# Decay weights of the state-space branch: the clipped difference formed by ScalarE, then one exponent of eight heads

## The chip, the cores and the metric

The kernel runs on one core of a Trainium2 chip. The metric is the device time of one execution in microseconds (us): the kernel before takes 2112.63 us, the median of three runs (2110.53 to 2113.01).

The engines are called PE (TensorE: matmuls and transposes), DVE (VectorE), ACT (ScalarE), POOL (GpSimd) and SP (SyncE, which issues the DMAs). PEld is the loading of PE's weights. Each engine takes its instructions strictly in the order in which they were written for it; an instruction that waits holds up all that stand behind it on its engine.

## The reference

A trunk of two layers. Each layer normalises its 1088 tokens (a prompt of 1024 and a sample of 64), projects them by one matrix, and sends column groups of the result through three branches: A, a gated linear recurrence; B, sparse attention, whose 256 keys per query are picked by an indexer score; C, a state-space scan (SSD). The three outputs are concatenated, projected back and added to the input. What the change touches lies in branch C:

```
cum   = cumsum(dt * a)                       # per chunk of tokens, per head
seg   = cum[l] - cum[s]
decay = exp(where(s <= l, seg, -inf))
wts   = decay * (C[l] . B[s]) * dt[s]
y     = wts @ x + (C @ h_prev) * exp(cum[l]) # and the state h moves on from chunk to chunk
```

## The kernel before

All tokens are worked on in chunks of 384, 384 and 320 columns, features on the partitions. A projection of 128 features is 72 matmuls (three per block of 128 inputs, since weights and activations are each split into a high and a low part, lines 235 to 237), and its weights are split by ACT (line 212, `whi`) and by POOL or DVE (line 213, `wlo`).

In the middle of each layer several things run side by side, and a plan string (`PLAN`) says in what order the program writes them:

- the projections for the state-space branch (`xbc`), each followed by a convolution of four taps (ACT line 872, POOL, DVE line 878), a tanh on ACT (line 887) and a product on DVE (line 888); gates (ACT line 431, DVE line 432); later the projections of branch A (`lru`);
- the selection of the keys (`select`), a binary search over the 31 bits of a threshold. Per bit DVE forms a candidate (line 622), DVE counts three score tiles against it (line 596), ACT counts four (line 602, `junka`), and DVE compares and keeps (lines 629 and 630). One bit is written after each projection, at a later priority;
- the scan (`ssd`), in 18 steps per layer (two head groups of eight heads, nine token tiles of 128 or 64). `ssd_inputs` prepares a step one step ahead of its use.

`ssd_inputs` loads the cumulative sums of eight heads, spread over all partitions, into `cumB` (partition: token s; columns: eight heads by 128 tokens l; DMA at line 730; two buffers). Then come eight DVE instructions, one per head, that subtract the head's column of `ctk` (cum[s], one number per partition) and cut at zero (line 760); one ACT exponent over all eight heads (line 763); one DVE product with the masked `C.B` (line 764). The result is the moving side of the 16 small matmuls at line 811, whose outputs DVE adds up (lines 807, 814, 815, 822). The inputs `xsc`, `bc` and `eB` of a step are DMAs too (lines 726, 728, 735), and PE transposes `xsc` at line 750.

The order of the instructions on each engine isn't the order of the program text. A scheduler places them by its own estimate of when each is ready, with the plan's order as priority, so that a change of one operation moves others. Buffers and semaphores follow from that order.

Of the kernel before, what the change touches and what calls it, by code (L numbers as in the profile page):

```python
# [14 lines left out]
AF = mybir.ActivationFunctionType  # L15
OP = mybir.AluOpType
# [56 lines left out]
def rows_of(t):  # L73
    return 128 if t < 8 else TS
# [14 lines left out]
def body(ctx, tc, I, O):  # L89
    nc = tc.nc  # L90
    V, G, S, PE, SP = nc.vector, nc.gpsimd, nc.scalar, nc.tensor, nc.sync

    def dram(x, off, ap):
        return bass.AP(tensor=x.tensor, offset=x.offset + off, ap=ap)
# [28 lines left out]
    def tp_bank():  # L123
        return bank("tp", 2)
# [175 lines left out]
    for l in range(DEPTH):  # L300
# [31 lines left out]
        with ExitStack() as st:  # L332
# [16 lines left out]
            for ci, (a, b) in enumerate(CH):  # L349
# [6 lines left out]
                for d in range(8):  # L356
# [3 lines left out]
                    else:  # L360
# [3 lines left out]
                                           op0=OP.mult, op1=OP.mult)  # L364
# [13 lines left out]
        dt, ctk, te, dec = [one.tile([128, NT, 16], F32, name=n) for n in ("dt", "ctk", "te", "dec")]  # L378
# [64 lines left out]
        g = nq = hl = None  # L443
# [28 lines left out]
        with ExitStack() as st:  # L472
# [38 lines left out]
            for j, zn in zip((6, 5, 4, 3, 2, 1, 0), IZ):  # L511
                fill(zn)
                t = j + 2
                n = rows_of(t)
# [14 lines left out]
                for c0 in range(0, nks[j], 512):  # L529
                    c1 = min(c0 + 512, nks[j])  # L530
                    for h in range(4):
# [5 lines left out]
                        if h == 0:  # L537
# [5 lines left out]
                                               op0=OP.mult, op1=OP.add)  # L543
# [20 lines left out]
            for t0, t1 in ((0, 4), (4, 8), (8, 9)):  # L564
                ps = tp_bank()
                w = 0
                for t in range(t0, t1):
                    n = rows_of(t)
# [148 lines left out]
        def ssd_inputs(g, tt):  # L717


            p = sa  # L720
            n = rows_of(tt)
            tok = tt * 128
            pad = tok + (3 if tt == 8 else 0)
            g8 = slice(8 * g, 8 * g + 8)
            xsc = p.tile([128, 4, 128], F32, name="xsc")
            SP.dma_start(xsc[:, :, :n], xsd[g][:, :, pad:pad + n])
            bc = p.tile([128, 2, 128], F32, name="bc")
            SP.dma_start(bc[:, :, :n], xsd[2][:, g:g + 3:2, pad:pad + n])
            cumB = p.tile([128, 8, 128], F32, name="cumB")
            SP.dma_start(cumB[:n, :, :n], cumd[None, g8, tok:tok + n].to_broadcast([n, 8, n]))  # L730
            eB = None
            if tt:
                eB = p.tile([128, 4, 128], F32, name="eB")
                for b in range(2):
                    SP.dma_start(eB[64 * b:64 * b + 64, :, :n],
                                 dram(cumd, (8 * g + b) * T + tok, [[0, 64], [2 * T, 4], [1, n]]))
                S.activation(eB[:, :, :n], eB[:, :, :n], AF.Exp)
            B_, C_ = bc[:, 0, :n], bc[:, 1, :n]

            ps = tp_bank()  # L740
            PE.matmul(ps[:n, :n], B_, C_, start=True, stop=True)
            PE.transpose(ps[:n, 128:256], B_, ident)
            cbm = p.tile([128, 128], F32, name="cbm")
            V.tensor_tensor(cbm[:n, :n], ps[:n, :n], triu[:n, :n], op=OP.mult)
            bt = p.tile([128, 128], F32, name="bt")
            S.activation(bt[:n], ps[:n, 128:256], AF.Copy)

            ps = tp_bank()
            for i in range(4):
                PE.transpose(ps[:n, i * 128:(i + 1) * 128], xsc[:, i, :n], ident)  # L750
            pv = ps[:n].rearrange("p (h c) -> p h c", h=8)
            xdt = p.tile([128, 8, 64], F32, name="xdt")
            V.tensor_tensor(xdt[:n], pv, dt[:n, tt, g8][:, :, None].to_broadcast([n, 8, 64]), op=OP.mult)
            xde = p.tile([128, 8, 64], F32, name="xde")
            G.tensor_tensor(xde[:n], xdt[:n], te[:n, tt, g8][:, :, None].to_broadcast([n, 8, 64]), op=OP.mult)
            G.tensor_tensor(xsc[:, :, :n], xsc[:, :, :n], dcol[:, 4 * g:4 * g + 4][:, :, None].to_broadcast([128, 4, n]),
                            op=OP.mult)

            for h in range(8):
                V.tensor_scalar(cumB[:n, h, :n], cumB[:n, h, :n], ctk[:n, tt, 8 * g + h:8 * g + h + 1], 0.0,  # L760
                                op0=OP.subtract, op1=OP.min)
            cB = cumB[:n, :, :n]
            S.activation(cB, cB, AF.Exp)
            V.tensor_tensor(cB, cB, cbm[:n, None, :n].to_broadcast([n, 8, n]), op=OP.mult)  # L764
            return xsc, C_, eB, bt, xdt, xde, cB

        def ssd(g):
            p = sa
            hT = None
            g8 = slice(8 * g, 8 * g + 8)  # L770
            order = [0, 1, 2, 3, 4, 5, 8, 6, 7]
            ready = ssd_inputs(g, 0)
            for k, tt in enumerate(order):
                ci = min(tt // 3, 2)
# [5 lines left out]
                if k + 1 < len(order):  # L780
                    ready = ssd_inputs(g, order[k + 1])
# [153 lines left out]
        g = [ssd(0), ssd(1)]  # L935
# [316 lines left out]
```

## Time and profile before

| | |
|---|---|
| median of 3 runs | 2112.63 us |
| profiled execution: its own time | 2118.68 us |
| its span | 2116.9 us |
| mean granted clock of PE | 0.98 |
| busy: PE, PEld, DVE, ACT, POOL | 93%, 84%, 76%, 54%, 31% |

The profiled execution is 6.05 us above the median. All times of the trace are from it. PE's busy share is modelled, and high all over; the shares of the other engines are means over stages that differ, so the stage in which the change lies has to be looked at by itself.

### The profile page before, as it was taken

The numbers are of one execution on the slowest core, as the hardware profiler recorded it, in microseconds if no ns is written. First come the engines' busy times: TensorE is split into PE (matmuls) and PEld (weight loads), VectorE is DVE, ScalarE is ACT, GpSimd is POOL, SyncE is SP. The second block draws the span as 40 slices with busy tenths as digits, with TensorE's granted clock in tenths as the row PEclk, the third lists the DMA queues.
The fourth block names the chain that finished last, engine by engine and source line by source line (L and its number), as shares of the span: only waits on it lengthen the run. The fifth ranks groups of instructions, "written<-read, shape, count | busy, mean of one in ns | idle before, by whom it ended". The sixth has DMA issues, their size and how long they took to land.

```text
span 2116.9 us, 34794 instructions
## 1 busy us (share of the span) xinstructions
PE 1975.6 (93%) x12076; PEld 1767.8 (84%) x12076; DVE 1614.3 (76%) x4102; ACT 1132.9 (54%) x2244; POOL 654.5 (31%) x561
## 2 busy tenths in 40 slices
PE   5989989888999899999999999988899998999999
PEld 5889988878898788866998999887888897888589
DVE  8668999999886875475287889999998778556723
ACT  5558967622465454445255798664324565444521
POOL 3012243433332332142430222443334225223420
PEclk9999999999999999999999999999999998999999
DMA  4135353353533642332641343534454326334145
GB/s 137 55 64 155 95 143 119 101 172 104 139 90 101 208 143 90 107 100 88 199 143 55 94 116 101 161 106 127 118 153 119 118 104 207 108 91 131 57 132 171
DMA packets 253368, 255.11 MB, mean 121 GB/s; under 512 B 31048, under 2 KB 233192, under 8 KB 253192
## 3 DMA queue, kind: packets, MB, share of 16 engines
q1 hardware_dynamic: 253192, 252.89, 39.9%
q8 instruction: 95, 1.56, 0.3%
q14 instruction: 81, 0.66, 0.1%
HBM read 176.68 MB, written 76.14 MB: 119 GB/s over the span
## 4 chain that ended last, share of the span: by engine, by line
PE 51%; DVE 29%; DMA 9%; issue 5%; ACT 3%; SPq 1%; POOL 1%; DVEq 0%; ACTq 0%; POOLq 0%
PE mm L236 12%; PE mm L237 12%; PE mm L235 11%; PE s L1119 4%; PE tp L1114 3%; PE s L1089 3%; DVE junk L596 3%; DVE u L878 3%; DMA cumB<-cumd 3%; DVE cumB L760 3%; DMA biasd<-g 2%; PE s L534 1%; PE s L904 1%; ACT junka L602 1%; DVE cumB L764 1%
## 5 line engine op out<-in xcount | busy, mean ns | idle before, releaser
L213 POOL TENSOR_TENSOR wlo<-wraw,whi 128x1024 fp32r<-128x1024 f32 x80 | 198.1, 2476 | 390.8 <-ACT whi L212 378.1
L602 ACT ACTIVATE junka<-sc,cand 128x768 bf16<-128x768 f32 x248 | 239.1, 966 | 24.7 <-DVE cand L622 20.6
L212 ACT ACTIVATE whi<-wraw 128x1024 fp32r<-128x1024 f32 x130 | 137.1, 1054 | 148.1 <-PE mm L236 89.3
L1096 ACT ACTIVATE lg<-lg,mx 128x512 f32<-128x512 f32 (+8 forms) x144 | 111.3, 773 | 108.8 <-DVE mx L1092 108.0
L1081 POOL TENSOR_TENSOR nbm<-nb,shared 128x256 f32<-128x256 f32 (+1 forms) x112 | 81.3, 729 | 231.1 <-DVE mx L1092 208.9
L878 DVE SCALAR_TENSOR_TENSOR u<-raw,parh,u 128x384 f32<-128x384 f32 (+1 forms) x198 | 144.7, 736 | 1.9 <-ACT u L872 0.8
L1116 ACT ACTIVATE pT<-tp 128x512 f32<-128x512 f32 (+1 forms) x164 | 90.2, 568 | 101.8 <-PE tp L1114 99.9
L596 DVE TENSOR_SCALAR_CACHE_REDUCE junk<-sc,cand 128x384 bf16<-128x384 f32 (+4 forms) x194 | 140.1, 752 | 0.7
L1089 PE MATMUL s<-kst,qst 128*128 128x512 f32 (+4 forms) x448 | 120.6, 361 | 9.7 <-DVE mx L1092 9.3
L1114 PEld LDWEIGHTS tp<-identr,lg 128*128 128x128 f32 (+2 forms) x656 | 71.8, 140 | 46.9 <-issue 39.7
L1114 PE MATMUL tp<-identr,lg 128*128 128x128 f32 (+2 forms) x656 | 107.3, 278 | 0.7 <-DVE lg L1099 0.7
L1119 PE MATMUL s<-pT,vt 128*64 128x256 f32 (+2 forms) x656 | 103.9, 392 | 1.6 <-ACT pT L1116 1.6
L1099 DVE TENSOR_SCALAR lg<-lg,ri 128x512 f32<-128x512 f32 (+8 forms) x144 | 98.1, 681 | 3.5
L760 DVE TENSOR_SCALAR cumB<-cumB,ctk 128x128 f32<-128x128 f32 (+1 forms) x288 | 83.3, 353 | 22.1 <-DMA cumB<-cumd 19.7
L1164 DVE TENSOR_TENSOR xl<-xl,mm 128x384 f32<-128x384 f32 (+1 forms) x40 | 21.4, 540 | 92.9 <-PE mm L237 84.7
L1089 PEld LDWEIGHTS s<-kst,qst 128*128 128x128 f32 (+1 forms) x448 | 71.5, 187 | 24.0 <-DVE mx L1092 16.4
L1092 DVE CUSTOM_DVE_ANT_0 lg<-s,shared 128x512 f32<-128x512 f32 (+4 forms) x112 | 61.8, 552 | 38.4 <-PE s L1089 32.4
L235 PE MATMUL mm<-sth0a,whi 128*128 128x384 f32 (+1 forms) x228 | 81.5, 360 | 7.8 <-DVE sth0a L974 2.6
L213 DVE TENSOR_TENSOR wlo<-wraw,whi 128x1024 fp32r<-128x1024 f32 x50 | 63.5, 1269 | 26.4 <-ACT whi L212 25.9
L236 PE MATMUL mm<-stl0a,whi 128*128 128x384 f32 (+1 forms) x228 | 79.6, 349 | 2.8 <-POOL stl0a L977 2.5
L798 POOL TENSOR_TENSOR hT<-hT,dec 128x512 f32<-128x512 f32 x28 | 40.7, 1454 | 131.4 <-DMA ycd<-yC 57.7
L236 PE MATMUL mm<-stl7a,whi 128*128 128x384 f32 (+1 forms) x228 | 78.6, 345 | 2.2 <-DVE stl7a L977 2.2
(477 smaller groups left out, 6977.5 us busy)
## 6 DMA issues: line engine op xcount, KB each, us to landing
wraw<-in_w_in_dram SPq DMA_DIRECT2D x82, 512.0 KB, 3.7
wraw<-in_w_out_dram SPq DMA_DIRECT2D x48, 512.0 KB, 4.2
cumB<-cumd SPq DMA_DIRECT2D x32, 512.0 KB, 5.2
xsd<-u SPq DMA_DIRECT2D x48, 192.0 KB, 2.3
gz<-gzd SPq DMA_DIRECT2D x32, 256.0 KB, 3.9
xsc<-xsd SPq DMA_DIRECT2D x32, 256.0 KB, 3.5
eB<-cumd SPq DMA_DIRECT2D x56, 128.0 KB, 3.5
gzd<-g SPq DMA_DIRECT2D x32, 192.0 KB, 1.9
```

The source lines that it names most:

```text
L212: S.activation(hi, raw, AF.Copy)
L213: eng.tensor_tensor(lo, raw, hi.bitcast(F32), op=OP.subtract)
L235: PE.matmul(ps, hi[:, k, :], xh[ci][:, c0:], start=k == 0, stop=False)
L236: PE.matmul(ps, hi[:, k, :], xl[ci][:, c0:], start=False, stop=False)
L237: PE.matmul(ps, lo[:, k, :], xh[ci][:, c0:], start=False, stop=k == len(xs) - 1)
L596: V.tensor_scalar(junk, sc[j][:n], thr, None, op0=op, op1=OP.add, accum_out=out)
L602: S.activation(junk, sc[j][:n], AF.Sign, scale=-1.0, bias=cand, accum_out=out)
L760: V.tensor_scalar(cumB[:n, h, :n], cumB[:n, h, :n], ctk[:n, tt, 8 * g + h:8 * g + h + 1], 0.0, op0=OP.subtract, op1=OP.min)
L878: V.scalar_tensor_tensor(u, raw[:, j:j + n], w[:, wbase + j * wstride:wbase + j * wstride + 1], u, op0=OP.mult, op1=OP.add)
L1089: PE.matmul(ps[:nq, :b - a], qst[:, h, :nq], kst[:, g, pt, kbase + a:kbase + b], start=pt == 0, stop=pt == 1)
L1114: PE.transpose(ps[:n, i * nq:(i + 1) * nq], lgs[h][:nq, j * 128:j * 128 + n], ident[:nq, :nq])
L1119: PE.matmul(av[64 * b:64 * b + 64, :, :nq], vt[:n, vj, 64 * g:64 * g + 64], pT[:n, 2 * b:2 * b + 2, :nq], start=j == 0, stop=j == nb_ - 1)
```

## The change

The eight DVE instructions of a step go. In their place stand eight ACT instructions: Relu(-1 * cumB + ctk column), which is max(ctk - cumB, 0), the clipped difference with its sign turned. The exponent takes the scale -1, which turns it back. Tiles, DMAs and the product at the end stay. Lines below this place have numbers that are one lower in the changed kernel (its exponent is line 762, the product line 763; the new Relu is line 761).

```
             for h in range(8):
-                V.tensor_scalar(cumB[:n, h, :n], cumB[:n, h, :n], ctk[:n, tt, 8 * g + h:8 * g + h + 1], 0.0,
-                                op0=OP.subtract, op1=OP.min)
-            cB = cumB[:n, :, :n]
-            S.activation(cB, cB, AF.Exp)
+                S.activation(cB[:, h, :], cB[:, h, :], AF.Relu, scale=-1.0, bias=ctk[:n, tt, 8 * g + h:8 * g + h + 1])
+            S.activation(cB, cB, AF.Exp, scale=-1.0)
             V.tensor_tensor(cB, cB, cbm[:n, None, :n].to_broadcast([n, 8, n]), op=OP.mult)
```

(`cB = cumB[:n, :, :n]` now stands ahead of the loop.) Over the program 288 DVE instructions become 288 ACT instructions: 256 of 128x128 and 32 of 64x64. The number of table loads on ACT stays at 17.

The scheduler's order moves with it. First DVE, in layer 0, where the scan's step with the tile `cumB_3592` is prepared. Before:

```order
L815 TENSOR_TENSOR yC_2901<-xsc_3062,eB_3068 128x4x128
L622 TENSOR_SCALAR cand_1564<-M_1563 128x7
L760 TENSOR_SCALAR cumB_3592<-cumB_3592,ctk_664 128x128 x5
L878 SCALAR_TENSOR_TENSOR u_3338<-raw_3335,parh_121,u_3338 128x384
L753 TENSOR_TENSOR xdt_3260<-tp_3255,dt_663 128x512
L760 TENSOR_SCALAR cumB_3592<-cumB_3592,ctk_664 128x128 x3
L822 SCALAR_TENSOR_TENSOR yC_2901<-yC_2901,gz_3275 128x4x128
L596 TENSOR_SCALAR junk_5258,cnt_1558<-sc0_698,cand_1564 128x384
```

The same place on DVE in the changed kernel:

```order
L814 TENSOR_TENSOR yC_2901<-xsc_3062,eB_3068 128x4x128
L877 SCALAR_TENSOR_TENSOR u_3338<-raw_3335,parh_121,u_3338 128x384
L821 SCALAR_TENSOR_TENSOR yC_2901<-yC_2901,gz_3275 128x4x128
L877 SCALAR_TENSOR_TENSOR u_3338<-raw_3335,parh_121,u_3338 128x384
L629 TENSOR_TENSOR keep_1565<-cnt_1558,lim_1560 128x7
L877 SCALAR_TENSOR_TENSOR u_3338<-raw_3335,parh_121,u_3338 128x384
L630 COPY_PREDICATED M_1563<-keep_1565,cand_1564 128x7
L622 TENSOR_SCALAR cand_1564<-M_1563 128x7
L596 TENSOR_SCALAR junk_5258,cnt_1558<-sc0_698,cand_1564 128x384
```

The eight subtractions are gone from between the step's sum (`yC`), the convolution (`u`) and the next bit's counts (`junk_5258`), and the convolution's instructions have moved up. Next ACT at the same step. Before:

```order
L212 ACTIVATE whi_3658<-wraw_3656 128x1024
L737 ACTIVATE eB_3594<-eB_3594 128x512
L862 ACTIVATE raw_3409<-mm_3384 128x256
L863 ACTIVATE raw_3409<-mm_3384 128x64
L763 ACTIVATE cumB_3592<-cumB_3592 128x1024
L824 ACTIVATE sq4_3300<-yC_2901 128x512
```

And in the changed kernel:

```order
L871 ACTIVATE u_3338<-raw_3335,parh_121 128x384
L602 ACTIVATE junka_5078,cnt_1558<-sc5_703,cand_1564 128x1024
L602 ACTIVATE junka_5080,cnt_1558<-sc6_704,cand_1564 64x576
L761 ACTIVATE cumB_3592<-cumB_3592,ctk_664 128x128 x7
L858 ACTIVATE raw_3372<-mm_3347 128x384
L761 ACTIVATE cumB_3592<-cumB_3592,ctk_664 128x128
L823 ACTIVATE sq4_3300<-yC_2901 128x512
L212 ACTIVATE whi_3658<-wraw_3656 128x1024
```

The eight Relus stand ahead of a copy out of a projection's bank (`raw_3372`) and of the split of the next weights (`whi_3658`), behind which the exponent of this tile follows some rows later.

## Rows read from the trace of the kernel before

**Rows 1.** the page: busy time by engine, shares of the last-ending chain.
```profile
PE 1975.6 (93%) x12076; PEld 1767.8 (84%) x12076; DVE 1614.3 (76%) x4102; ACT 1132.9 (54%) x2244; POOL 654.5 (31%) x561
...
PE 51%; DVE 29%; DMA 9%; issue 5%; ACT 3%; SPq 1%; POOL 1%; DVEq 0%; ACTq 0%; POOLq 0%
PE mm L236 12%; PE mm L237 12%; PE mm L235 11%; PE s L1119 4%; PE tp L1114 3%; PE s L1089 3%; DVE junk L596 3%; DVE u L878 3%; DMA cumB<-cumd 3%; DVE cumB L760 3%; DMA biasd<-g 2%; PE s L534 1%; PE s L904 1%; ACT junka L602 1%; DVE cumB L764 1%
```

**Rows 2.** stretches: length; busy us of PE, PEld, DVE, ACT, POOL; clock, DMA.
```profile
250.00:450.00 200.00, 178.95 (x1106) 166.75 (x1105) 193.03 (x478) 125.53 (x255) 74.44 (x57) 0.96 0.43 126
450.00:660.00 210.00, 196.93 (x1206) 179.19 (x1205) 180.88 (x410) 85.94 (x150) 75.35 (x60) 0.98 0.42 121
1300.00:1480.00 180.00, 158.40 (x996) 145.72 (x994) 173.57 (x430) 113.27 (x228) 72.11 (x54) 0.98 0.42 124
1480.00:1690.00 210.00, 195.04 (x1202) 178.29 (x1202) 187.55 (x424) 84.23 (x146) 76.07 (x60) 0.98 0.43 125
```

**Rows 3.** the same stretches, busy time of line 760 on DVE alone.
```profile
250.00:450.00 200.00, 22.85 (x64) 0.96 0.43 126
450.00:660.00 210.00, 16.02 (x64) 0.98 0.42 121
1300.00:1480.00 180.00, 19.03 (x56) 0.98 0.42 124
1480.00:1690.00 210.00, 18.68 (x72) 0.98 0.43 125
sum 800.00, DVE 76.58; mean DVE 19.15
```

**Rows 4.** chain of waits, 250 to 500, 500-660, 1290-1500, 1500-1680.
```profile
by line: DVE junk L596 10.6%; DVE u L878 9.5%; issue 9.4%; DVE cumB L760 9.1%; DMA cumB<-cumd 6.1%; ACT junka L602 3.6%; DMA xsc<-xsd 3.1%; DMA bc<-xsd 3.0%; DVE sc L656 2.9%; DVE u L888 2.8%; DVE cumB L764 2.7%; DVE yC L815 2.7%; DVE g L43
...
by line: issue 11.5%; DMA cumB<-cumd 8.3%; PE mm L236 5.4%; PE mm L237 5.3%; PE s L904 5.3%; PE mm L235 5.1%; DVE wlo L213 4.2%; DVE cumB L760 3.4%; DVE xc L878 3.1%; DVE thl L917 2.8%; DVE cumB L764 2.5%; DVE yC L837 2.3%; DMA eB<-cumd 2.1
...
by line: DVE u L878 12.3%; DVE junk L596 11.0%; issue 8.6%; DMA cumB<-cumd 8.6%; DVE cumB L760 8.4%; ACT junka L602 4.2%; DVE u L888 3.8%; DVE cumB L764 3.8%; DMA bc<-xsd 3.5%; DVE yC L815 2.9%; DVE sc L605 2.9%; DVE g L432 2.7%; DVE M L630
...
by line: issue 12.5%; DMA cumB<-cumd 8.9%; DVE cumB L760 5.8%; DVE wlo L213 4.3%; DVE sc L656 3.9%; PE s L904 2.9%; DVE rs_tq L179 2.9%; DVE xc L878 2.8%; PE mm L237 2.6%; PE mm L236 2.5%; DVE thl L917 2.4%; PE mm L235 2.4%; DVE cumB L764 2
```

**Rows 5.** groups by shape: xcount | busy us, mean ns | idle before, releasers.
```profile
L760 DVE TENSOR_SCALAR cumB<-cumB,ctk 128x128 f32<-128x128 f32 x256 | 73.0, 349 | 15.9 <-DMA cumB<-cumd 13.6 <-issue 2.0
L760 DVE TENSOR_SCALAR cumB<-cumB,ctk 64x64 f32<-64x64 f32 x32 | 10.3, 389 | 6.1 <-DMA cumB<-cumd 6.1
...
L763 ACT ACTIVATE cumB<-cumB 128x1024 f32<-128x1024 f32 x32 | 33.9, 1058 | 69.0 <-DVE cumB L760 69.0
L872 ACT ACTIVATE u<-raw,parh 128x384 f32<-128x384 f32 x48 | 33.7, 702 | 11.8 <-DMA xsd<-u 8.0 <-DVE junk L653 3.3
L1096 ACT ACTIVATE lg<-lg,mx 128x128 f32<-128x128 f32 x16 | 6.3, 394 | 3.0 <-DVE mx L1092 2.5 <-DVE ri L1098 0.5
```

**Rows 6.** line 760: ns min/median/max, its waits, and who waited for it.
```profile
L760 DVE TENSOR_SCALAR cumB<-cumB,ctk x288: 236/276/4418, 178.4 to 1665.8; 128x128 f32<-128x128 f32 x128, 64x64 f32<-64x64 f32 x16
...
  DMA cumB<-cumd: 19.7, 13
...
  ACT cumB L763: 79.1, 26
```

**Rows 7.** DVE in order of time, two steps: start us, us, what.
```profile
365.09 3.75 DVE L760 TENSOR_SCALAR cumB<-cumB,ctk 64x64 f32<-64x64 f32 x8
...
408.16 1.65 DVE L760 TENSOR_SCALAR cumB<-cumB,ctk 128x128 f32<-128x128 f32 x8
```

**Rows 8.** POOL in order of time, 360 to 371.
```profile
364.18 1.29 POOL L755 TENSOR_TENSOR xde<-xdt,te 128x512 f32<-128x512 f32 x1 [3.64 <-DVE xdt L753]
365.44 2.38 POOL L213 TENSOR_TENSOR wlo<-wraw,whi 128x1024 fp32r<-128x1024 f32 x1
```

**Rows 9.** ACT in order of time, two instructions in a row.
```profile
554.53 0.69 ACT L872 ACTIVATE xc<-raw,pk 128x384 f32<-128x384 f32 x1
555.13 0.60 ACT L875 ACTIVATE u<-raw,pk 128x384 f32<-128x384 f32 x1
```

**Rows 10.** who waited for whom: us in total, times, longest.
```profile
PE tp L750 <- DMA xsc<-xsd: 31.1, 19, 3.1
```

**Rows 11.** the page: the DMA of line 730, KB and us to landing.
```profile
cumB<-cumd SPq DMA_DIRECT2D x32, 512.0 KB, 5.2
```

More of the change, by code (lines that the diff above doesn't have):

```diff
@@ L757, in ssd_inputs @@
                             op=OP.mult)
+            cB = cumB[:n, :, :n]
             for h in range(8):
-                V.tensor_scalar(cumB[:n, h, :n], cumB[:n, h, :n], ctk[:n, tt, 8 * g + h:8 * g + h + 1], 0.0,
-                                op0=OP.subtract, op1=OP.min)
-            cB = cumB[:n, :, :n]
-            S.activation(cB, cB, AF.Exp)
+                S.activation(cB[:, h, :], cB[:, h, :], AF.Relu, scale=-1.0, bias=ctk[:n, tt, 8 * g + h:8 * g + h + 1])
+            S.activation(cB, cB, AF.Exp, scale=-1.0)
             V.tensor_tensor(cB, cB, cbm[:n, None, :n].to_broadcast([n, 8, n]), op=OP.mult)
```

## The prediction

> **What bounds the kernel now.** I read the page first, then busy time by stretches, then line 760 within them, then the chain of waits in each, and last the single instructions.
>
> The page [rows 1] makes PE look like the bound: 93% busy and 51% of the chain that ended last. But DVE holds 29% of that chain, and the removed line alone 3% of it (which is 57 us, from the parts below). A mean over the span hides where. So cut out the middle of each layer, where the scan runs. There are two kinds of stretch in it [rows 2]. In 250 to 450 and 1300 to 1480 (the search stretches: state-space projections, key search, scan of the first head group) DVE is busy 193.03 of 200 us and 173.57 of 180, that is 96.5% and 96.4%. PE is at 178.95 (89%) and 158.40 (88%), ACT at 125.53 and 113.27 (63%). In 450 to 660 and 1480 to 1690 (the end of the search, the scan of the second group, branch A) PE leads with 196.93 and 195.04 of 210 (94%, 93%), DVE has 180.88 and 187.55, ACT 85.94 and 84.23. So DVE bounds the first kind, and in the second PE works between short waits for DVE, DMAs and others.
>
> Line 760 takes 22.85, 16.02, 19.03 and 18.68 us of these four, 76.58 of its 83.3 in all [rows 3, 5]. It is also on the chain that decides: 9.1% of 250 us and 8.4% of 210 in the search, 3.4% of 160 and 5.8% of 180 behind it [rows 4], so 22.8 + 17.6 + 5.4 + 10.4 = 56.2 us.
>
> **The change part by part.**
>
> Removed from DVE: 288 instructions, 73.0 + 10.3 = 83.3 us busy [rows 5]. How much of that can return as DVE time has two bounds. An undisturbed group of eight takes 1.65 us [rows 7], and 36 of them 59 us. The other 24 us are stretching: the shortest instruction takes 236 ns, the longest 4418 [rows 6], and the group that began at 365.09 took 3.75 us for tiles of a quarter of the size, while POOL was running its two products from 364.18 to 367.82 without a pause [rows 7, 8]. That time could simply be passed on to the next DVE instruction, which then meets the same POOL work. So 59 to 83 us; I take 75, nearer to the measured sum, since the instruction behind 760 is often one that reads PSUM or is late anyway. Besides, DVE stood 19.7 us at line 760 for the DMA of `cumB` with its queue behind it [rows 6]; that wait moves to ACT, and DVE has other work.
>
> The Trainium skill (GPSIMD Engine Reference, 1. Specifications) says that GpSimd's SBUF interfaces are shared with VectorE, with contention for instructions in a two-port mode or with two SBUF inputs. The trace agrees as far as the two rows above go; by that rule the products at lines 764 and 815 would inherit some of the stretching, and the sum would lie at the 59 us end.
>
> Added on ACT: 288 Relus with a column as bias. The trace has no such instruction. Nearest is line 1096 at 128x128: SBUF to SBUF, f32, an exponent with a column as bias, 394 ns [rows 5]. In a row they cost less: line 872 lasts 0.69 us, and the next begins 0.60 us after it [rows 9], so some 0.1 us overlap. That makes 0.29 us each, 2.35 us a group, 85 us in all if the 32 small ones are priced alike. From above, without overlap, 113 us. From below, the pace of line 760 itself, 0.21 us each (1.65/8), 59 us. I take 85, since the nearest row is of the same engine and shape.
>
> What lies beside other work. In the search stretches 64 and 56 instructions move, and ACT goes to 125.5 + 18.8 = 144 of 200 and 113.3 + 16.4 = 130 of 180, both 72%. In the other two it goes to 105, below PE. So there is room on ACT everywhere, and the step is prepared a step ahead: in the order of the changed kernel the Relus of a tile stand many rows ahead of the product that needs it. The exponent itself waited 79.1 us for line 760 [rows 6]. That wait becomes ACT's own work.
>
> What is queued behind the new wait. The first Relu of a step now waits on ACT for the DMA of `cumB`, 5.2 us from issue to landing [rows 11]. Behind it on ACT stand the copies out of the projections' banks (`raw`), the split of the weights (`whi`) and the counts of the search (`junka`); PE waits for the first two, DVE for the last. With the load issued a step ahead it has mostly landed; where DVE found it late, it was 13 times, 1.5 us on average. Bounds: 0 to 19.7 us on the path. I take 3.
>
> Not touched: DMAs, matmuls, POOL, the number of table loads.
>
> **The sum.** In the search stretches, take DVE's 22.85 and 19.03 us away, and the busiest engine is PE. If the stretch stays as much longer than its busiest engine as now, 200/193.03 x 178.95 = 185.4 and 180/173.57 x 158.40 = 164.3, a gain of 14.6 + 15.7 = 30.3 us. But three engines are then close together (in 185 us PE at 96%, DVE with 170 us at 92%, ACT with 144 at 78%), each in its fixed order, and the hand-overs cost more than with one clear leader. I take two thirds, 20 us. Behind the search PE leads already, and only its waits can shrink: line 760 has 15.8 us of the chain there. Other waits stand ready for its place, above all the landing of `xsc`, for which PE waited 31.1 us in all [rows 10], so I take 8. The 3 us of ACT's new wait go against it. Sum: 20 + 8 - 3 = 25, and some 2 us for what frees up outside of the four stretches (83.3 - 76.6 = 6.7 us of the line). 27 us off the profiled execution's 2118.68 is 2092; the median of the runs lies 6 us below that execution, so **2085 us**, 1.3% faster.
>
> **The rivals.**
>
> A, all of it comes through. The 56 us on the chain go, and nothing takes their place: 2112.6 - 56 = 2057. For it: PE is idle 800 - 729.3 = 70.7 us in the four stretches [rows 2], so there is that much to give back, and its clock stands at 0.96 to 0.98 there, which could rise if its pauses shrink. Against: all waits of PE would have to go, those for DMAs too.
>
> B, nothing comes through. The place of line 760 is taken by the next wait at once: `cumB`'s and `xsc`'s landings, which hang on the buffers of the step before, or PE's own order, which the scheduler has changed around it. For it: the landing of `cumB` is on the chain with 6.1 to 8.9% in every stretch [rows 4], as much as the line itself. Against: at 96% DVE leaves no room for another bound in the search. Time 2108 to 2117.
>
> C, slower: ACT's queue gets onto the path. The place is the search. One bit goes from DVE to four counts on ACT and back, and ACT's counts are already 3.6 and 4.2% of the chain [rows 4]; a group of Relus in front of them, of a bank's copy, or of `whi`, delays each by up to 2.35 us. With all 36 groups on the path 85 us come and 56 go: 2112.6 + 29 = 2141. It decides from two thirds of the groups on (36 x 56/85 = 24). For it: in the changed order seven Relus stand right ahead of a bank's copy and the eighth ahead of the next `whi`. Against: ACT stays at 72%, and 63% now leaves it 74 us idle in the first search stretch.
>
> The Trainium skill speaks for C (ScalarE: Activation LUTs, Rules for kernel authors): it tells to give relu, max and add to VectorE and not to ScalarE. The rows above agree on the price, 1.65 us a group on DVE and 2.35 on ACT. By that rule alone, with both engines on the path, the change would cost 36 x 0.7 = 25 us, 2138.
>
> **How the numbers follow.** The forecast (a gain of 10 to 45 us) 0.50; A (over 45) 0.12; B (a gain of 10 to a loss of 5) 0.17; C 0.21. About 0.2%, 4.2 us, is what a measurement of this kernel can tell from no change. Of B I count 0.06 as faster by more than that, 0.10 as the same and 0.01 as slower. So faster 0.68, same 0.10, slower 0.22. For the range I leave out half of A below (0.06) and the end of C above (0.12): 2055 to 2128. The likeliest case's own range is 2068 to 2103.
>
> **What would show it.** In the profile after: DVE's busy time lower by 59 to 83 us, ACT's higher by about 85, a Relu of 0.38 to 0.40 us with groups of eight in 2.2 to 2.5 us. In the stretches of the search DVE some 85 to 90% busy, PE above 91%, and the stretches 8 to 12 us shorter each. The chain there without line 760, and with little of the new line 761. POOL's stretching: if lines 764 and 815 get longer on average, the 24 us were passed on. The prediction is wrong if ACT's Relu line carries several per cent of the chain there (C), or if PE's busy share there stays at 89% with the wait for `xsc` or `cumB` grown (B).

## The result, and the profile after

The changed kernel takes 2083.96 us, the median of four runs (2081.34 to 2088.56); the kernel before takes 2112.82 in the same comparison (2110.53 to 2114.15). The ratio is 0.9867, with a 95% interval of 0.9845 to 0.9889: 1.3% faster, 28.9 us. The profiled execution of the changed kernel takes 2081.64 us, its span is 2079.8.

The page of the changed kernel, busy time by engine and the chain that ended last, against [rows 1]:

```profile
PE 1967.7 (95%) x12076; PEld 1765.5 (85%) x12076; DVE 1530.5 (74%) x3814; ACT 1209.4 (58%) x2532; POOL 646.1 (31%) x561
...
PE 62%; DVE 18%; DMA 10%; issue 4%; ACT 3%; POOL 1%; SPq 1%; DVEq 0%; ACTq 0%; POOLq 0%
PE mm L235 14%; PE mm L236 14%; PE mm L237 14%; PE s L1118 4%; PE tp L1113 4%; PE s L1088 3%; DMA cumB<-cumd 2%; DMA biasd<-g 2%; PE s L534 1%; DVE u L877 1%; DMA xsc<-xsd 1%; PE s L903 1%; DVE junk L596 1%; DVE sc L656 1%; DVE cumB L763 1%
```

DVE lost 83.8 us of work and ACT gained 76.5. On the chain DVE went from 29% to 18%, and PE from 51% to 62%; neither ACT's share nor the DMAs' grew by more than one point. PE stood still for 2116.9 - 1975.6 = 141.3 us before and for 2079.8 - 1967.7 = 112.1 us now. So 29.2 of the 37.1 us between the two spans are pauses of PE that are gone, and the rest is less of PE's own busy time, as the trace models it. (The two profiled executions lie further apart than the medians.)

The same four stretches of the clock as in [rows 2] (length; busy us of PE, PEld, DVE, ACT, POOL; clock, DMA):

```profile
250.00:450.00 200.00, 191.63 (x1233) 179.72 (x1232) 191.07 (x448) 153.19 (x345) 84.34 (x65) 0.99 0.49 146
450.00:660.00 210.00, 195.63 (x1189) 178.77 (x1188) 169.19 (x342) 109.52 (x215) 70.66 (x56) 0.98 0.37 108
1300.00:1480.00 180.00, 171.07 (x1096) 159.93 (x1094) 174.22 (x398) 136.30 (x309) 80.89 (x63) 0.98 0.51 151
1480.00:1690.00 210.00, 201.50 (x1229) 184.26 (x1230) 167.22 (x334) 114.44 (x213) 64.79 (x53) 0.98 0.36 109
```

In 250 to 450 PE does 1233 matmuls where it did 1106, and is busy 96% instead of 89%. DVE is still busy 95.5%, with other work: the stretch has filled up. That is to be kept in mind whenever one cuts by the clock, for a stretch doesn't hold the same work in both kernels. Behind the search PE was at 94% and 93% and is at 93% and 96% now.

What the moved work costs, by shape (xcount | busy, mean ns | idle before, and what ended it), and its neighbours:

```profile
L877 DVE SCALAR_TENSOR_TENSOR u<-raw,parh,u 128x384 f32<-128x384 f32 x132 | 96.8, 742 | 5.8 <-ACT u L871 3.4 <-POOL u L875 1.8
L761 ACT ACTIVATE cumB<-cumB,ctk 128x128 f32<-128x128 f32 x256 | 80.4, 391 | 46.7 <-DMA cumB<-cumd 45.7 <-PE mm L237 1.0
L763 DVE TENSOR_TENSOR cumB<-cumB,cbm 128x1024 f32<-128x1024 f32 x32 | 48.2, 1507 | 2.2 <-ACT cumB L762 2.0
L762 ACT ACTIVATE cumB<-cumB 128x1024 f32<-128x1024 f32 x32 | 33.6, 1050 | 0.0
...
L814 DVE TENSOR_TENSOR yC<-xsc,eB 128x512 f32<-128x512 f32 x28 | 23.6, 842 | 0.1
```

A Relu takes 391 ns, and the next one begins before it is over. Eight of them span 2.45 us on ACT's timeline (start us, us, what, idle before):

```profile
388.59 2.45 ACT L761 ACTIVATE cumB<-cumB,ctk 128x128 f32<-128x128 f32 x8 [1.95 <-DMA cumB<-cumd]
```

The exponent's wait of 69.0 us [rows 5] is gone, and in its place stands a wait of the first Relu for the load of `cumB`, 45.7 us. The chain of waits in the stretches of [rows 4] says what these are worth (250 to 500, 500 to 660, 1290 to 1500, 1500 to 1680):

```profile
by line: PE mm L235 10.7%; PE mm L237 10.5%; PE mm L236 10.5%; issue 8.7%; DVE u L877 5.2%; DVE junk L596 4.4%; DVE sc L656 4.3%; DMA xsc<-xsd 4.0%; DVE cumB L763 3.6%; DMA cumB<-cumd 3.2%; DVE junk L658 2.7%; DVE junk L653 1.9%; DVE junk L
...
by line: DMA cumB<-cumd 13.2%; PE mm L236 11.5%; PE mm L235 11.5%; PE mm L237 11.4%; PE s L903 6.9%; issue 5.1%; ACT cumB L761 3.9%; DVE xc L877 2.5%; DVE yC L836 2.3%; DMA xsc<-xsd 2.0%; DVE thl L916 1.9%; PE s L810 1.9%; DVE wlo L213 1.6%
...
by line: PE mm L235 9.5%; PE mm L236 9.3%; PE mm L237 9.3%; issue 8.6%; DVE u L877 6.2%; DVE junk L596 5.3%; DVE sc L656 4.6%; DVE cumB L763 4.2%; DMA xsc<-xsd 4.2%; DVE junk L658 2.9%; DVE junk L653 2.3%; DVE junk L659 1.8%; DVE u L887 1.8
...
by line: PE mm L235 10.9%; PE mm L237 10.8%; PE mm L236 10.5%; DMA cumB<-cumd 8.3%; PE s L903 6.9%; issue 3.9%; ACT cumB L761 3.9%; DVE xc L877 2.9%; DVE yC L836 2.6%; PE s L810 2.5%; DMA xsc<-xsd 2.0%; PE s L805 2.0%; DMA eB<-cumd 1.9%; PE
```

In the search stretches the projections' matmuls (lines 235 to 237) lead the chain now, with 31.7% and 28.1%; before, lines of DVE did. The Relus are not among the lines shown there, and the load of `cumB` has shrunk from 6.1% to 3.2% in the first. Behind the search it is otherwise. Load and difference together had 8.3 + 3.4% of 160 us and 8.9 + 5.8% of 180, that is 45 us; load and Relu now have 13.2 + 3.9% of 160 and 8.3 + 3.9% of 180, that is 49 us. The stretches of the clock don't hold quite the same work in both kernels, but by these sums the wait there has only changed its engine.

### The profile page after: what moved, and what is told of

Read it like the earlier page. It is cut to its first block, busy times and chain, and to the rows that moved or that the text cites. A ratio compares the mean times of both kernels' runs of the same rounds, so it can differ in the third digit from the quotient of the medians.

```text
span 2079.8 us, 34780 instructions
## 1 busy us (share of the span) xinstructions
PE 1967.7 (95%) x12076; PEld 1765.5 (85%) x12076; DVE 1530.5 (74%) x3814; ACT 1209.4 (58%) x2532; POOL 646.1 (31%) x561
## 4 chain that ended last, share of the span: by engine, by line
PE 62%; DVE 18%; DMA 10%; issue 4%; ACT 3%; POOL 1%; SPq 1%; DVEq 0%; ACTq 0%; POOLq 0%
PE mm L235 14%; PE mm L236 14%; PE mm L237 14%; PE s L1118 4%; PE tp L1113 4%; PE s L1088 3%; DMA cumB<-cumd 2%; DMA biasd<-g 2%; PE s L534 1%; DVE u L877 1%; DMA xsc<-xsd 1%; PE s L903 1%; DVE junk L596 1%; DVE sc L656 1%; DVE cumB L763 1%
## 5 line engine op out<-in xcount | busy, mean ns | idle before, releaser
L877 DVE SCALAR_TENSOR_TENSOR u<-raw,parh,u 128x384 f32<-128x384 f32 (+1 forms) x198 | 132.5, 677 | 7.6 <-ACT u L871 3.4
L761 ACT ACTIVATE cumB<-cumB,ctk 128x128 f32<-128x128 f32 (+1 forms) x288 | 88.5, 385 | 48.3 <-DMA cumB<-cumd 47.3
L235 PE MATMUL mm<-sth0a,whi 128*128 128x384 f32 (+1 forms) x228 | 83.3, 367 | 15.4 <-DVE g L432 9.8
L1098 DVE TENSOR_SCALAR lg<-lg,ri 128x512 f32<-128x512 f32 (+8 forms) x144 | 90.3, 630 | 3.2
L236 PE MATMUL mm<-stl1a,whi 128*128 128x384 f32 (+1 forms) x228 | 80.2, 352 | 1.1 <-DVE stl1a L976 1.1
L237 PE MATMUL mm<-sth3a,wlo 128*128 128x384 f32 (+1 forms) x228 | 80.8, 355 | 0.0
```

The costliest lines, as they stand in the source:

```text
L235: PE.matmul(ps, hi[:, k, :], xh[ci][:, c0:], start=k == 0, stop=False)
L236: PE.matmul(ps, hi[:, k, :], xl[ci][:, c0:], start=False, stop=False)
L237: PE.matmul(ps, lo[:, k, :], xh[ci][:, c0:], start=False, stop=k == len(xs) - 1)
L877: V.scalar_tensor_tensor(u, raw[:, j:j + n], w[:, wbase + j * wstride:wbase + j * wstride + 1], u, op0=OP.mult, op1=OP.add)
```

## The experiments

Each was timed in five rounds beside the kernel before on the same chip, whose medians were 2114.74 us (the first four), 2116.86 (the next four) and 2116.20 (the last four). Single runs of the kernel before lay between 2107.87 and 2122.67, so single profiled executions are read here for where time goes, and not for a few us of the total. The added instructions of four of the kernels compute something that nothing reads.

**DVE's work given back, waiting for nothing.**

```
+            spare = p.tile([128, 128], F32, name="spare", bufs=1)
+            for h in range(8):
+                V.tensor_scalar(spare[:n, :n], triu[:n, :n], ctk[:n, tt, 8 * g + h:8 * g + h + 1], 0.0,
+                                op0=OP.subtract, op1=OP.min)
             for h in range(8):      # the Relus, as changed
```

> The changed kernel, with eight further subtract-and-clip instructions of the old form on DVE per scan step, from a constant tile into a spare tile that nobody reads: DVE has about the old load again (288 x 0.21 = 59 us undisturbed, 83 with stretching), but none of it waits for the load of cumB or stands between the load and the exponent. Theory 1 (the gain is DVE time in the middle of the layer): most of the gain is lost, 2100 to 2115 us. Theory 2 (the gain comes from the order into which the scheduler put the other instructions): it changes by chance, 2070 to 2100. Theory 3 (the gain is the wait for cumB's load, which no longer holds up DVE's queue): the gain stays, 2082 to 2090.

2115.44 us, ratio 0.9998 [0.9984, 1.0012]: all of the gain is gone. The added line of this kernel, by shape:

```profile
L762 DVE TENSOR_SCALAR spare<-triu,ctk 128x128 f32<-128x128 f32 x256 | 110.5, 432 | 1.9
```

The stretch 250 to 450 of the same kernel:

```profile
250.00:450.00 200.00, 181.45 (x1146) 167.05 (x1144) 192.75 (x486) 153.93 (x344) 78.39 (x60) 0.99 0.46 134
```

And its chain from 250 to 500:

```profile
by line: issue 13.6%; DVE u L881 10.0%; DVE junk L596 8.9%; DVE spare L762 7.5%; ACT junka L602 4.5%; DVE sc L656 2.8%; DMA cumB<-cumd 2.8%; DVE u L891 2.4%; DVE junk L658 2.1%; DVE M L630 2.0%; DMA eB<-cumd 2.0%; DMA xsc<-xsd 1.9%; PE mm L
```

DVE's total is 1614.2 us, as before (1614.3), PE falls back to 91%, and the projections' lines fall behind DVE's on the chain. The dependence of the exponent on DVE is not there in this kernel, and the wait for `cumB` stands on ACT, as in the changed one. So the gain is DVE's time, and not the shorter chain of dependences. Nor is it PE's granted clock: it rose from 0.96 to 0.99 in this stretch with the change, and it is 0.99 here too, without any gain.

**The Relus doubled on ACT.**

```
+            spare = p.tile([128, 128], F32, name="spare", bufs=1)
+            for h in range(8):
+                S.activation(spare[:n, :n], triu[:n, :n], AF.Relu, scale=-1.0, bias=ctk[:n, tt, 8 * g + h:8 * g + h + 1])
```

> The changed kernel, with eight further Relus per scan step on ACT, from a constant tile into a spare tile that nobody reads: some 85 us more on ACT, which goes from 153 to about 175 of 200 us in the first search stretch. Theory 1 (ACT has room, the Relus lie beside other work): a small part of the 85 us shows, 2086 to 2100. Rival (ACT is already on the path, the gain is what is left over after a cost of the Relus): at least half of the 85 us shows, 2125 or more.

2119.74 us, ratio 1.0020 [1.0008, 1.0032]: by the two ratios some 32 us slower than the changed kernel, for 1302.7 - 1209.4 = 93 us more on ACT. But the search itself goes on as well as before: in 250 to 450 PE is busy 193.85 us, more than in the changed kernel:

```profile
250.00:450.00 200.00, 193.85 (x1248) 180.77 (x1247) 182.46 (x416) 176.61 (x419) 90.80 (x68) 1.00 0.50 144
```

The loss is behind it, in one place in each layer. In the first (stretches of 25 us, this kernel):

```profile
450.00:475.00 25.00, 25.00 (x155) 23.99 (x154) 24.91 (x80) 20.51 (x57) 2.57 (x2) 1.00 0.21 73
475.00:500.00 25.00, 21.15 (x154) 18.41 (x152) 24.91 (x48) 17.76 (x48) 12.17 (x10) 1.00 0.61 169
500.00:525.00 25.00, 0.59 (x2) 0.50 (x2) 25.00 (x50) 7.85 (x17) 6.29 (x3) 0.55 0.36 102
525.00:550.00 25.00, 24.42 (x137) 22.57 (x138) 16.38 (x45) 6.54 (x14) 3.27 (x3) 0.91 0.28 83
```

PE's longest wait of this kernel between 495 and 530 (total, times, longest):

```profile
PE s L281 <- DVE dg L279: 19.4, 1, 19.4
```

In the second layer the same wait stands between 1480 and 1660:

```profile
PE s L281 <- DVE dg L279: 19.4, 1, 19.4
```

And the chain of the first layer from 500 to 525:

```profile
by line: DVE sc L656 28.2%; DVE junk L596 15.6%; DVE junk L659 14.5%; DVE junk L658 9.9%; DVE junk L653 8.9%; DVE wlo L213 4.5%; DVE shared L660 4.3%; issue 3.1%; DVE yC L824 2.4%; DVE rs_tq L180 2.2%; DVE rs_yq L181 2.1%; DVE need L655 1.0
```

The last bit's last count on ACT begins at 446.3 us (396.5 in the changed kernel), on an ACT that is now 88% busy in the search (176.61 of 200 us). The masks that close the search (lines 653 to 660) then run on DVE up to 527 us. Between them, in DVE's order, stand the small instructions of a norm (lines 175 to 181), which end in one that PE needs (line 279), and PE is idle for 19.4 us. So ACT's load can use up the gain, at twice the load; with the load of the change the masks are over at 492 us, and PE doesn't stand there. Late counts alone don't do this: with DVE's wait put back and with the exponent cut in two (both below) the last count begins at 419.5 and 418.8 us, and both keep the gain.

**The order alone, on both kernels.** The decay step is written ahead of the `C.B` matmul; nothing else changes. On the changed kernel (on the kernel before the same lines with its own loop; in both, the lines go from their old place below):

```
+            cB = cumB[:n, :, :n]
+            for h in range(8):
+                S.activation(cB[:, h, :], cB[:, h, :], AF.Relu, scale=-1.0, bias=ctk[:n, tt, 8 * g + h:8 * g + h + 1])
+            S.activation(cB, cB, AF.Exp, scale=-1.0)
             B_, C_ = bc[:, 0, :n], bc[:, 1, :n]
```

> The kernel before with the subtract loop and the exponent written earlier in the step, ahead of the matmul of C and B: the same instructions on the same engines, so that only the scheduler's order differs. Theory 1: 2105 to 2120, as before. Theory 2 (order is what decides): it moves by 15 us or more, either way.

> The changed kernel with the Relus and the exponent written earlier in the step, ahead of the matmul of C and B: the same work as in the changed kernel, only the order differs. Theory 1: 2075 to 2095, the gain stays. Theory 2: the gain of the changed kernel was one draw of an order, and this one may lie anywhere between 2070 and 2130.

The kernel before: 2114.74 us, ratio 1.0002 [0.9992, 1.0012]. The changed kernel: 2078.62, ratio 0.9827 [0.9812, 0.9842], against 0.9867 [0.9845, 0.9889] unmoved; the two intervals lie 0.0003 apart and come from two comparisons, so a small gain is likely, some 8 us. This move of the order explains nothing of the 28.9 us. What the scheduler reorders by itself when the engine changes isn't tested by it. It is the fastest version measured.

**Half of the heads.** Heads 0 to 3 on ACT, 4 to 7 on DVE, an exponent for each half:

```
-            for h in range(8):
+            for h in range(4):
                 S.activation(cB[:, h, :], cB[:, h, :], AF.Relu, scale=-1.0, bias=ctk[:n, tt, 8 * g + h:8 * g + h + 1])
-            S.activation(cB, cB, AF.Exp, scale=-1.0)
+            for h in range(4, 8):
+                V.tensor_scalar(cB[:, h, :], cB[:, h, :], ctk[:n, tt, 8 * g + h:8 * g + h + 1], 0.0,
+                                op0=OP.subtract, op1=OP.min)
+            S.activation(cB[:, 0:4], cB[:, 0:4], AF.Exp, scale=-1.0)
+            S.activation(cB[:, 4:8], cB[:, 4:8], AF.Exp)
```

> Heads 0 to 3 of a step on ACT (Relu), heads 4 to 7 on DVE as before, and two exponents of four heads (36 more ACT instructions, about 0.2 us each). Half the DVE time returns (30 to 42 us). Theory 1 (DVE time in the search is the limit, the gain grows with what is taken off): about half the gain, 2095 to 2104. Rival (gain stops as soon as DVE is no longer the last, a little is enough): all of it, 2080 to 2088.

2112.82 us, ratio 0.9980 [0.9967, 0.9993]: 4 us, where half would be 14. The stretch 250 to 450:

```profile
250.00:450.00 200.00, 178.89 (x1129) 166.75 (x1128) 190.60 (x462) 140.25 (x308) 76.49 (x60) 0.96 0.47 136
```

PE is busy as it was before (178.95). By the table at the end it is nevertheless 15 us ahead at 446 us, and loses most of that lead in the next 50.

**One head group at a time.** The loop chooses the engine by `g == 0`, or by `g == 1`:

```
+                if g == 0:
                     S.activation(cB[:, h, :], cB[:, h, :], AF.Relu, scale=-1.0, bias=ctk[:n, tt, 8 * g + h:8 * g + h + 1])
+                else:
+                    V.tensor_scalar(cB[:, h, :], cB[:, h, :], ctk[:n, tt, 8 * g + h:8 * g + h + 1], 0.0,
+                                    op0=OP.subtract, op1=OP.min)
-            S.activation(cB, cB, AF.Exp, scale=-1.0)
+            S.activation(cB, cB, AF.Exp, scale=-1.0 if g == 0 else 1.0)
```

> Only the first head group of a layer (the 9 steps that run mainly beside the key search, 250 to 450 us) has the clipped difference on ACT; the second group has it on DVE as before. Theory 1, as predicted (20 of the 27 us come from the search stretches, 8 from behind): 2088 to 2098. Rival (the gain comes where the search ends and branch A begins, with the second group): 2105 to 2114.

> Only the second head group of a layer (the 9 steps that run mainly after the search's bits) has the clipped difference on ACT. Theory 1, as predicted: a small part of the gain, 2102 to 2110. Rival: most of it, 2085 to 2098. If both groups alone give less than the whole, they add up; if either alone gives it all, one limit was behind both.

Group 0 alone: 2090.94 us, ratio 0.9886 [0.9870, 0.9902], 24 of the 28.9 us. Group 1 alone: 2117.68, ratio 1.0007 [0.9994, 1.0020], nothing. Whether group 1 adds the 4 us that are left once group 0 is moved can't be told: the intervals of group 0 alone and of the whole change overlap. Group 0 is the one that is scanned during the search, as the stretch 250 to 450 shows, here of the kernel with group 0 on ACT:

```profile
250.00:450.00 200.00, 190.42 (x1214) 178.60 (x1213) 191.26 (x448) 147.14 (x322) 87.43 (x67) 0.97 0.50 144
```

And here of the one with group 1 on ACT, where PE is as it was before:

```profile
250.00:450.00 200.00, 178.62 (x1104) 165.75 (x1104) 192.58 (x473) 126.24 (x258) 74.90 (x57) 0.96 0.43 126
```

**A third buffer for `cumB`**, with the moved order, so that the load can start a step earlier:

```
-            cumB = p.tile([128, 8, 128], F32, name="cumB")
+            cumB = p.tile([128, 8, 128], F32, name="cumB", bufs=3)
```

> The changed kernel with the Relus written earlier in the step (as in the run before), and a third buffer for cumB, so that its load can start a step earlier. In the changed kernel ACT stood 47 us at the first Relu for that load, and behind the search the load is 13% of the chain of waits. Theory 1 with that wait as the next limit: 2062 to 2074. Rival (the wait on ACT is idle time off the path, or the load is held by SP's queue and not by the buffer): 2075 to 2084, no change against the two-buffer kernel's 2079.

2096.48 us, ratio 0.9905 [0.9889, 0.9921]: by the two ratios 16 us slower than with two buffers. ACT's wait for the load did fall, from 44.8 to 19.3 us. The chain from 250 to 500 has `junka` with 5.9%:

```profile
by line: issue 7.3%; PE mm L237 7.0%; PE mm L236 6.7%; PE mm L235 6.5%; DVE u L877 6.3%; DVE junk L596 6.0%; ACT junka L602 5.9%; DMA cumB<-cumd 5.3%; DVE sc L656 2.8%; ACT cumB L740 2.7%; DVE cumB L763 2.7%; DVE u L887 2.3%; DMA xsc<-xsd 2
```

The last bit's last count begins at 423.7 us instead of 395.4. It is tempting to call this the cause: the Relus, no longer held back, would run ahead of the search's counts. But the next kernel below, which keeps the gain whole, has its last count at 419.5 and even more `junka` on that chain:

```profile
by line: DVE u L879 10.4%; issue 9.3%; DMA cumB<-cumd 8.5%; ACT junka L602 6.7%; DVE junk L596 6.4%; DVE cumB L765 4.1%; ACT cumB L763 3.6%; DVE sc L656 3.4%; DVE g L432 2.3%; DVE junk L658 2.3%; DVE u L889 2.2%; DMA xsc<-xsd 2.1%; DMA xsd<
```

So the later search isn't shown to be what costs the 16 us. The table at the end shows where they go: the lead in the search is smaller (16 us at 446 against 28), and 11 us of it are lost right behind each search. By which wait stays open.

**DVE's wait for the load put back, without its work.** DVE copies one column of `cumB` per step and so stands in its queue until the load has landed:

```
+            spare = p.tile([128, 1], F32, name="spare", bufs=1)
+            V.tensor_copy(spare[:n], cumB[:n, 0, 0:1])
             for h in range(8):      # the Relus
```

> The changed kernel, with one tiny DVE copy per step (one column of cumB into a spare column that nobody reads) ahead of the Relus: DVE's queue stops again for the load of cumB, and the Relus wait for DVE, but DVE has only some 5 us more to do. Theory 1 (DVE's busy time in the search is the limit): the gain stays, 2080 to 2092. Theory 3 (it counts that DVE's queue no longer stops for that load, which would explain why half of the heads gave only 4 us): at least half of the gain is lost, 2100 to 2115.

```profile
L761 DVE COPY spare<-cumB 128x1 f32<-128x1 f32 (+1 forms) x36 | 5.2, 144 | 17.2 <-DMA cumB<-cumd 17.2
```

DVE waits 17.2 us there (19.7 in [rows 6]), and the time is 2084.57, ratio 0.9847 [0.9832, 0.9862]: the gain is whole. Putting that wait back costs nothing.

**Half of DVE's work given back** (four added instructions a step instead of eight), and **every second token tile on ACT** (five of nine steps):

```
+            spare = p.tile([128, 128], F32, name="spare", bufs=1)
+            for h in range(4):
+                V.tensor_scalar(spare[:n, :n], triu[:n, :n], ctk[:n, tt, 8 * g + h:8 * g + h + 1], 0.0,
+                                op0=OP.subtract, op1=OP.min)
```
```
+            on_act = tt % 2 == 0
             for h in range(8):
+                if on_act:
                     S.activation(cB[:, h, :], cB[:, h, :], AF.Relu, scale=-1.0, bias=ctk[:n, tt, 8 * g + h:8 * g + h + 1])
+                else:
+                    V.tensor_scalar(cB[:, h, :], cB[:, h, :], ctk[:n, tt, 8 * g + h:8 * g + h + 1], 0.0,
+                                    op0=OP.subtract, op1=OP.min)
-            S.activation(cB, cB, AF.Exp, scale=-1.0)
+            S.activation(cB, cB, AF.Exp, scale=-1.0 if on_act else 1.0)
```

> The changed kernel, with four (not eight) further subtract-and-clip instructions per step on DVE, from a constant tile, waiting for nothing: half the load of the first run. Theory 1, linear: half of the gain is lost, 2094 to 2104. A threshold (the search is either bound by DVE or not): all of it is lost, 2108 to 2116, or none, 2080 to 2090. With theory 3: none.

> The clipped difference is on ACT in the steps of even token tiles (5 of 9 steps of each group), on DVE in the others: 56% of the work is moved, as in the run with half of the heads, but whole steps at a time, so that in 5 of 9 steps nothing on DVE waits for the load of cumB, and without a second exponent. Theory 1, linear: 56% of the gain, 2094 to 2102. Theory 3: the same, since half of the waits go. A threshold: under 6 us of gain, 2107 to 2114, as with half of the heads.

2117.74 us, ratio 1.0006 [0.9994, 1.0017], and 2111.28, ratio 0.9975 [0.9962, 0.9987]. Neither keeps its share of the gain. With half of the added work the search still goes faster than before, but at 510 to 530 PE stands, 8 of 20 us (stretch of the kernel with four added instructions):

```profile
510.00:530.00 20.00, 11.89 (x70) 9.82 (x71) 17.17 (x34) 11.25 (x27) 13.07 (x10) 0.74 0.53 140
```

In the changed kernel it doesn't:

```profile
510.00:530.00 20.00, 20.00 (x137) 19.59 (x136) 18.15 (x48) 9.54 (x23) 6.06 (x5) 1.00 0.49 137
```

**The exponent cut in two** on the changed kernel, which the half-heads kernel has as well:

```
-            S.activation(cB, cB, AF.Exp, scale=-1.0)
+            S.activation(cB[:, 0:4], cB[:, 0:4], AF.Exp, scale=-1.0)
+            S.activation(cB[:, 4:8], cB[:, 4:8], AF.Exp, scale=-1.0)
```

> The changed kernel with the exponent of a step cut in two of four heads each, as the run with half of the heads had it: 36 more ACT instructions, 36 x 0.15 = 5 us on ACT. If the second exponent was not what spoiled the run with half of the heads: 2080 to 2092. If it was: 2100 or more.

2084.02 us, ratio 0.9857 [0.9833, 0.9880]: the second exponent costs nothing, so it isn't what spoilt the half-heads kernel.

**Where the lead is won and lost.** PE runs the same number of matmuls in all kernels, 12076, so its progress can be compared by count, though not matmul by matmul, since the scheduler orders them differently. The heading is a time in the kernel before. The table counts how many matmuls PE has started there by then, and gives the time at which the other kernel starts its matmul of the same number, less the time in the kernel before (us, from the starts in the traces; negative is ahead). In the first layer, 446 and 500 lie at the end of the search, where its masks are formed in the kernel before, 559 and 600 right behind it, 692 and 765 on the way into attention. In the second, most of the steps of the scan that run beside the search begin after 1300; 1488 and 1500 lie at its end, 1550 and 1600 right behind it.

```
                    446  500  559  600  692  765 1300 1488 1500 1550 1600 2037
changed             -27  -20  -21  -21  -18  -15  -20  -45  -39  -40  -43  -36
  moved             -28  -21  -23  -21  -19  -17  -22  -46  -38  -39  -42  -36
  exponent in two   -21  -22  -14  -17  -16  -16  -20  -41  -40  -42  -33  -36
  DVE waits         -18  -15  -14  -15  -15  -13  -17  -34  -29  -30  -32  -34
group 0 only        -28  -20  -15  -16  -17  -14  -18  -43  -37  -36  -34  -30
third buffer        -16  -18   -7   -9  -11  -12  -17  -30  -30  -32  -21  -23
ACT doubled         -25  -29   -5   -5   -3    1   -1  -22  -21  -28   -2   -4
DVE half load       -12  -13   -5   -6   -2    2    2  -11   -7   -9   -2   -2
half heads          -15   -6   -7   -8    2    3    6   -9    0   -2   -3   -1
five of nine        -12   -3   -3   -2   -3    0   -5  -15   -9   -9   -5   -5
group 1 only         -1   -1   -1   -2    1    1   -3   -2   -3   -3   -6   -4
DVE full load        -8   -5   -3   -3   -4   -3   -4   -9   -4   -7   -3    0
before, moved        -4   -2   -1   -1    1    1   -3   -1   -2   -3   -3   -4
```

Each row is one execution. The last one, where only the order differs and the time is that of the kernel before, shows differences of up to 4 us by itself, so a few us mean nothing. Three things stand out.

Nearly all of the lead is made in the search, in both layers: the changed kernel is 27 us ahead at 446, and it goes from 20 at 1300 to 45 at 1488.

There the lead goes with the work taken off DVE. At 446 it is 27 us with nothing given back, 12 with half and 8 with all; with half of the heads and with five of nine steps moved it is 15 and 12. From 1300 to 1488 it is 25, 13 and 5, and 15 and 10.

Much of it can be lost right behind. Doubled ACT loses 24 us between 500 and 559, and 26 between 1550 and 1600, at its two long waits. The changed kernel loses 7 us between 446 and 500, which leaves it 20; half of the heads and five of nine steps lose 9 there, which leaves them 6 and 3, and half of DVE's load loses 8 between 500 and 559, which leaves it 5. Half of the heads has single waits of PE there, in both layers, for the landing of `xsc`; five of nine steps has one for a gate on DVE (start us, us, what, idle before):

```profile
447.97 1.11 PE L750 MATMUL tp<-identr,xsc 128*128 128x128 f32 x4 [9.22 <-DMA xsc<-xsd]
1489.85 1.12 PE L750 MATMUL tp<-identr,xsc 128*128 128x128 f32 x4 [7.28 <-DMA xsc<-xsd]
448.48 0.69 PE L235 MATMUL mm<-sth0a,whi 128*128 128x384 f32 x1 [5.55 <-DVE g L432]
```

The longest of the changed kernel between 440 and 500 is 3.6 us. So far the traces account for the small worth of the partial moves: they make about half of the lead, and what is lost behind the search is no smaller for them. No run took these waits away to prove it. Nor does the size of the lead alone decide: with DVE's wait put back it is 18 us at 446, little more than with the third buffer, and all of the gain is kept.

## Why the prediction came out right, and where it didn't

The time was forecast at 2085 and is 2083.96. Step by step:

- **DVE bounds the search, and its time is what counts**: shown. Giving DVE the work back takes all of the gain, without any of the dependences; putting back the wait alone takes nothing; the order alone gives nothing; and PE's lead in the search goes with the work taken off DVE.
- **75 us less on DVE (59 to 83)**: 83.8, the upper end: DVE's other lines together changed by half a us. Lines 764 and 815 were named as heirs of the stretching; the products take 1507 ns instead of 1564 and 842 instead of 839, and the convolution 742 instead of 793. The Trainium skill's rule on the interfaces that DVE and GpSimd share (GPSIMD Engine Reference, 1. Specifications) would have passed some of it on to the products; these rows don't show that. Other lines moved far in both directions, though, as two of them show (the first of each pair is the kernel before):

```profile
L605 DVE TENSOR_SCALAR sc<-sc,sg 128x384 f32<-128x384 f32 (+6 forms) x28 | 24.0, 888 | 0.0
L605 DVE TENSOR_SCALAR sc<-sc,sg 128x384 f32<-128x384 f32 (+6 forms) x28 | 14.9, 570 | 0.0
L864 DVE COPY stc<-raw 128x3 f32<-128x3 f32 x32 | 12.7, 398 | 1.3 <-ACT raw L862 1.2
L863 DVE COPY stc<-raw 128x3 f32<-128x3 f32 x32 | 24.0, 752 | 6.8 <-ACT raw L861 6.8
```

So DVE's instructions are still stretched, now at other places. The total shows that none of the 24 us came back on balance, and not that none was passed on.

- **0.29 us a Relu, 2.35 us a group, 85 us in all**: 2.45 us a group and 88.5 us for the line; the single Relu is 391 ns, as its neighbour's 394 said. ACT's total rose by 76.5 only. Nothing was saved elsewhere: no other line of ACT became shorter by more than half a us, apart from two table loads that moved to another line. The 12 us are time in which the records of two instructions on ACT overlap, which the engine's total counts once and the lines count twice.
- **30.3 us in the search, of which two thirds**: the size is right partly by luck. Group 0 alone gives 24 us where 20 were taken. In the search itself PE gains more than forecast, 20 us by 500 and 19 from 1300 to 1500, against 14.6 and 15.7. The third was taken off for hand-overs within the search; the losses that the table shows lie behind it. And the time doesn't scale as the lead does: by the 28.9 us for 83.8 us of DVE, half of the load given back should have kept 11 us (DVE is 31.5 below before), and it kept none.
- **8 us behind the search**: too high. Group 1 alone gives nothing, on top of group 0 some 4 us that the intervals don't tell from nothing, and the chain there holds 49 us of load and Relu where it held 45. PE was already the leader, and the wait for `cumB` changed its engine. In the sum this error and the one before it cancelled.
- **0 to 19.7 us for ACT's new wait, 3 taken**: the bound was wrong, the wait is 47.3 us over all steps. ACT stood there 22 times, DVE 13 times. In the first search the load is on the chain with 3.2%, from 6.1%; behind the search it is on it with 13.2% and 8.3%, and belongs to the point above.
- **Room on ACT everywhere, 72% in the search**: too wide. It is 77% and 76%, because the stretches filled up. With the Relus doubled, ACT's load costs all of the gain. It does so in the masks behind the search and not in the search itself, where rival C had put it. Rival C lost by the size of the load.
- **Signs that were named**: PE above 91% in the search (96% and 95%), no Relu on the chain there: seen. DVE at 85 to 90%: not seen, it is at 95.5% and 97%, with more work done in the same time. The stretches shorter by 8 to 12 us each: more, by the 20 and 19 us above. Lines 764 and 815 longer: not seen.

The Trainium skill's advice to give relu to VectorE and not to ScalarE (ScalarE: Activation LUTs, Rules for kernel authors) speaks of the price of the operation, and there the trace agrees in direction, 2.45 us a group against 1.65. By that price alone, on all 36 groups, the change would lose 29 us; it wins 28.9, since the dearer engine isn't the one that bounds the search.

## What to carry to other kernels

Work moved off the engine that is 96% busy in a stage pays even where the other engine needs half as much again, but only in that stage: the same move in the stage next to it, alone, gave nothing. Test such a claim by giving the engine its time back with work that waits for nothing, and test the wait, the order and the time apart. Expect no proportion in the time: half of the move made half of the lead here, and the waits behind the stage took as much from it as from the whole. So measure the whole change before dropping it for what half of it did.

## What was not expected

A kernel with the longer wait can be the faster one: with a third buffer ACT waited 19.3 us instead of 44.8, and the kernel became 16 us slower; why isn't shown. DVE's total fell by 83.8 us, all of the line's 83.3, and not only by the 59 of 36 undisturbed groups, although single lines elsewhere on DVE became longer. And DVE instructions that do the same on tiles that no one waits for were longer still, 432 ns on average against 349.
